# A decoder step on one core: the gate's decay made earlier on ScalarE, and the first loads and a polynomial put elsewhere

## The chip, the core and the metric

The kernel runs on one core of a Trainium2 chip. The metric is the device time of one execution in microseconds (us); lower is better. Engines are named as the profile names them: PE (TensorE products), PEld (TensorE weight loads), DVE (VectorE), ACT (ScalarE), POOL (GpSimd), SP (SyncE, which only issues DMAs here).

## What is computed

One layer of a hybrid decoder, for 256 prompt tokens and 8 x 4 sample tokens together, with the same weights. Cut to what matters here:

```
h  = rmsnorm(x, g)
xr, gr, q, kvc, kvs, kvw, g_nsa, g_m = split_in(h @ w_in)
# recurrent branch (RG-LRU)
xc = causal_dwconv(xr);  r, i = sigmoid(xc @ wa + ba), sigmoid(xc @ wx + bx)
log_a = -8 * r * softplus(-lam);  a = exp(log_a)
u = sqrt(-expm1(2 * log_a)) * (i * xc)
h_t = a_t * h_(t-1) + u_t;  y_rnn = h_t * gelu(gr)
# attention branch on q and the keys and values, then gates, w_out, a conv FFN, a last rmsnorm
```

The kernel writes t = tanh(r * 4 * softplus(-lam)), so that a = (1 - t) / (1 + t) = 2 / (1 + t) - 1 and sqrt(1 - a^2) = 2 sqrt(t) / (1 + t).

## The kernel before

All activations lie transposed: 128 features on the partitions, 288 tokens along the rows. A 128 x 1024 block of weights (8 tiles of 128 x 128) is loaded as `raw` and split into two parts in a shorter float format: `wh`, a copy made by ACT (line 161), and `wl`, the rest, made by DVE (line 162, on a few blocks by POOL). The activations are split in the same way into `hh` and `hl`. Each tile then takes three products of 288 columns (lines 179, 180, 181: wh by hh, wh by hl, wl by hh), so one block is 24 products. A block's work is called a step here.

`load_w` keeps the split two blocks ahead of the products: at the start of step i it puts the split of block i + 2 into the queues of ACT and DVE. There are 3 buffers for `wh`, 3 for `wl` and 4 for `raw`; the copy of block i + 2 waits until PE has finished with block i - 1. SP issues all weight loads in order. Every engine works through its queue strictly in program order, and that order is written by hand: `run` walks through units of steps, and `at(n, f)` puts the side function `f` behind step n of the walk.

Places that the change touches:

- The start (lines 285 to 340). `wake` sends 8 products of ones through PE. Then 8 chunks `c` of two feature blocks each are loaded: `x_load(c)` issues x (line 295) and the weights `wkc` (line 297). Chunk 0 goes in two halves, the others whole. The first half of chunk 0's weights is issued by ACT, all else by SP; the norm's vector `vec` (line 299) goes on SP behind the first half of x. `norm_in` makes `hh` on ACT (line 233, scaled by `vec`) and `hl` on DVE (line 234). For chunk 0 all products wh by hh come first, then wh by hl, then wl by hh (line 334); from chunk 1 on the three follow each other tile by tile. POOL issues the loads of the sample states `st` and `h0` (lines 358, 359) in its first microseconds.
- `r_lam1` (lines 392 to 401): a polynomial for softplus(-lam), 17 DVE instructions on 128 x 8 elements, the last of which writes `sp4`. It stands behind the norm's scale `dg` (lines 262 to 264) and ahead of the next two splits of weights on DVE. `xr_out(0)` (lines 374, 375) comes behind these splits and empties the PSUM bank that the unit after next fills.
- The recurrent branch runs as side work: for each of the 8 blocks j, `r_gate1` (sigmoids and tanh on ACT, then B = 1 + t on POOL) stands behind step 3j + 5 of the walk and `r_gate2` (B = 1 / B, line 496, DVE) behind 3j + 7. `r_sqrt` (ACT, line 499) stands behind steps 27 and 28, `r_gelu` (ACT, line 502) behind 29 and 30. `r_scan0(j)` behind step 28 + j and `r_scan1(j)` behind 29 + j are the scan stage: two DVE operations for u (lines 505, 506), then on ACT a = 2B - 1 in the place of B (line 507), then the scan itself on DVE (line 510). In that stage the units are the queries, and `unit_q` adds one DVE operation (line 447) at every second step.

Of the kernel before, what the change touches and what calls it, by code (L numbers as in the profile page):

```python
# [87 lines left out]
def body(ctx, tc, a, o):  # L88
# [196 lines left out]
    xcm, xp = pool("xp", side="right")  # L285
    acc = new_acc()
    acc2 = q_sb[:, 0:2]
    wake(psg(), 8)
    kz = [psb(), psb(), pst(), pso()]

    def x_load(c):
        xc = xp.tile([P, 2, N], F32, tag="xc", name="xc", bufs=8)
        raw = w_tiles(None)
        for ks in ((0, 1), (1, 2)) if c == 0 else ((0, 2),):
            nc.sync.dma_start(xc[:, ks[0]:ks[1]], a["x"][:, 2 * c + ks[0]:2 * c + ks[1]])
            first = c == 0 and ks[0] == 0
            (nc.scalar if first else nc.sync).dma_start(raw[:, 4 * ks[0]:4 * ks[1]], a["wkc"][c][:, 4 * ks[0]:4 * ks[1]])
            if first:
                nc.sync.dma_start(vec[:, V_GM:V_GM + KD], a["vec"][:, V_GM:V_GM + KD])
        if c == 5:  # L300
            nc.sync.dma_start(vec[:, KD:], a["vec"][:, KD:])
            nc.sync.dma_start(cs, a["cst"])
        return xc, raw
# [9 lines left out]
    for c in range(8):  # L313
        xc, raw = x_load(c)
        if c == 0:
            S.activation(warm, mhalf, AF.Copy)
        wh, wl = w_parts(raw)
        for k2 in range(2):
            k = 2 * c + k2
            norm_in(xc[:, k2], vcol(V_GM, k), hh[:, k], hl[:, k])  # L320
            if c == 0:
                split(wh[:, 4 * k2:4 * k2 + 4], wl[:, 4 * k2:4 * k2 + 4], raw[:, 4 * k2:4 * k2 + 4])
            elif k2 == 0:
                split(wh, wl, raw)
        if prev is not None and c > 1:
            V.tensor_add(acc2, acc2, prev)
        prev = x_squares(c, xc)
        for k2 in range(2):
            k = 2 * c + k2
            if c == 0:  # L330

                for n, (w, x) in enumerate(((wh, hh), (wh, hl), (wl, hh))):
                    for j in range(4):
                        T.matmul(kz[j][:, :N], w[:, 4 * k2 + j], x[:, k], start=k == 0 and n == 0, stop=False)
            else:
                for j in range(4):
                    mm3(kz[j][:, :N], wh[:, 4 * k2 + j], wl[:, 4 * k2 + j], hh[:, k], hl[:, k], False, k == KD - 1)
# [17 lines left out]
    B = rp.tile([P, RB, RW], F32, name="B")  # L355
    C = rp.tile([P, RB, RW], F32, name="C")
    orn = rp.tile([P, RB, 36], F32, name="orn")
    nc.gpsimd.dma_start(st, a["rcs"])
    nc.gpsimd.dma_start(h0, a["rh0"])
    rb = None  # L360

    def samp(t):
# [47 lines left out]
        pass  # L410
    rms_sum(qn, acc, True, True)
    dg = rms_diag(qn)
    r_lam1()
    g = unit(qx[1][:, :N], 2, hh, hl)
    next(g)
    qb = rms_bcast(dg)
# [78 lines left out]
    def r_gate2(j):  # L495
        V.reciprocal(B[:, j, :RC], B[:, j, :RC])

    def r_sqrt(j):
        S.activation(A[:, j:j + 2, :RC], A[:, j:j + 2, :RC], AF.Sqrt)

# [1 line left out]
        S.activation(gr[:, j:j + 2], gr[:, j:j + 2], AF.Gelu_apprx_tanh)  # L502

    def r_scan0(j):
        V.scalar_tensor_tensor(A[:, j, :RC], A[:, j, :RC], 2.0, B[:, j, :RC], op0=ALU.mult, op1=ALU.mult)
        V.tensor_mul(A[:, j, :RC], A[:, j, :RC], C[:, j, :RC])
        S.activation(B[:, j, :RC], B[:, j, :RC], AF.Identity, scale=2.0, bias=mone)

    def r_scan1(j):
        V.tensor_tensor_scan(C[:, j, :NP], B[:, j, :NP], A[:, j, :NP], 0.0, op0=ALU.mult, op1=ALU.add)  # L510
# [24 lines left out]
        side.setdefault(n, []).append(lambda: f(*args))  # L535

    for j in range(RB):
        for i, f in ((0, r_conv0), (1, r_conv1), (2, r_parts), (3, r_gate0), (4, r_gate1), (6, r_gate2)):
            at(3 * j + 1 + i, f, j)
        at(28 + j, r_scan0, j)  # L540
        at(29 + j, r_scan1, j)
        at(38 + j // 2, r_out0, j)
        at(39 + j // 2, r_out1, j)
    for i in range(4):
        at(27 + i // 2, r_sqrt, 2 * i)
        at(29 + i // 2, r_gelu, 2 * i)
# [709 lines left out]
```

## Time and profile before

| | us |
|---|---|
| median of 3 runs | 1673.66 (1673.54 to 1673.69) |
| profiled execution, its own time | 1674.1 |
| its span in the profile | 1672.3 |
| PE busy | 1645.1 (98%) |
| DVE busy | 1017.5 (61%) |
| ACT busy | 765.3 (46%) |

A busy PE in the profile is not a PE at its peak, since products are pipelined and their ends are modelled. Whether PE loses time is read from the starts of its products: in the undisturbed stretches one product of 288 columns starts 0.13 us behind the other. A stretch with fewer starts than that has lost time, and the row of the product that starts late names in brackets what it waited for.

### The profile page before, as it was taken

To read this page: it belongs to the slowest core of one execution; us is meant where nothing else is said; L and a number is where in the kernel's file an instruction comes from. 1 tells how busy PE (TensorE), PEld (TensorE's weight loads), DVE (VectorE), ACT (ScalarE), POOL (GpSimd) and SP (SyncE) were. 2 spreads that over 40 slices of the span, in tenths; PEclk is the share of its full clock that TensorE was granted. 3 is DMA by queue.
4 is the path that set the end of the run, shared out by engine and by line. 5 is a ranking of instruction groups with operands and counts; after the bars stand their busy time and mean duration, and the time that the engine had idled before them with its cause. 6 is when DMAs were issued, how large, how long until landed. Compare 5 with 4: busy or idle time off the path is not lost.

```text
span 1672.3 us, 31396 instructions
## 1 busy us (share of the span) xinstructions
PE 1645.1 (98%) x12722; PEld 1634.0 (98%) x12722; DVE 1017.5 (61%) x1544; ACT 765.3 (46%) x1091; POOL 247.2 (15%) x427
## 2 busy tenths in 40 slices
PE   9999999999999999999999999999999999999997
PEld 9999999899999999999999999999999999999997
DVE  6776867787775555666566556444456556654443
ACT  6555555565554444444444444333344444443332
POOL 0341100541440001330000000000000000001112
PEclk9999999999999999999999999999999999999999
DMA  7554585544556555555566655555555555555553
GB/s 269 178 170 132 156 295 175 157 144 153 171 169 212 164 174 167 167 169 159 172 200 205 198 163 167 172 171 165 167 163 165 175 163 166 174 175 175 157 175 107
DMA packets 88371, 290.79 MB, mean 174 GB/s; under 512 B 10178, under 2 KB 19154, under 8 KB 88098
## 3 DMA queue, kind: packets, MB, share of 16 engines
q1 hardware_dynamic: 85394, 276.73, 54.5%
q0 software_dynamic: 1968, 10.45, 1.9%
q8 instruction: 100, 1.64, 0.4%
q10 hardware_dynamic: 864, 1.59, 0.3%
q14 instruction: 45, 0.37, 0.1%
HBM read 284.02 MB, written 8.85 MB: 175 GB/s over the span
## 4 chain that ended last, share of the span: by engine, by line
PE 87%; DVE 6%; ACT 3%; issue 2%; POOL 1%; DMA 1%; SPq 0%; POOLq 0%; ACTq 0%; DVEq 0%
PE ps_g L179 28%; PE ps_g L181 27%; PE ps_g L180 27%; DVE wl L162 2%; PE ps_b L601 1%; DVE k L176 1%; ACT wh L161 1%; DVE mx L803 1%; DVE pr L806 1%; ACT pr L798 1%; DMA raw<-in_wkc_dram 0%; ACT k L175 0%; DVE pr L790 0%; POOL rest L859 0%; PE ps_b L181 0%
## 5 line engine op out<-in xcount | busy, mean ns | idle before, releaser
L162 DVE TENSOR_TENSOR wl<-raw,wh 128x1024 fp32r<-128x1024 f32 (+1 forms) x481 | 595.1, 1237 | 468.7 <-ACT wh L161 467.8
L161 ACT ACTIVATE wh<-raw 128x1024 fp32r<-128x1024 f32 (+1 forms) x497 | 523.4, 1053 | 362.7 <-PE ps_g L180 265.0
L179 PE MATMUL ps_g<-h2h,wh 128*128 128x288 f32 x1536 | 451.0, 294 | 0.0
L180 PE MATMUL ps_g<-h2l,wh 128*128 128x288 f32 x1536 | 450.8, 293 | 0.0
L181 PE MATMUL ps_g<-h2h,wl 128*128 128x288 f32 x1536 | 449.7, 293 | 0.0
L179 PE MATMUL ps_g<-hh,wh 128*128 128x288 f32 x1024 | 304.6, 297 | 1.2 <-DVE xr L375 0.7
L181 PE MATMUL ps_g<-hh,wl 128*128 128x288 f32 x1024 | 300.9, 294 | 4.3 <-DVE wl L162 4.3
L180 PE MATMUL ps_g<-hl,wh 128*128 128x288 f32 x1024 | 300.9, 294 | 0.0
L181 PEld LDWEIGHTS ps_g<-h2h,wl 128*128 128x128 f32 x1536 | 289.4, 188 | 0.0
L179 PEld LDWEIGHTS ps_g<-h2h,wh 128*128 128x128 f32 x1536 | 288.4, 188 | 0.1
L180 PEld LDWEIGHTS ps_g<-h2l,wh 128*128 128x128 f32 x1536 | 288.4, 188 | 0.1
L180 PE MATMUL ps_g<-gl,wh 128*128 128x288 f32 x768 | 225.4, 293 | 0.0
L179 PE MATMUL ps_g<-gh,wh 128*128 128x288 f32 x768 | 225.4, 293 | 0.0
L181 PE MATMUL ps_g<-gh,wl 128*128 128x288 f32 x768 | 224.8, 293 | 0.0
L181 PEld LDWEIGHTS ps_g<-hh,wl 128*128 128x128 f32 x1024 | 192.9, 188 | 5.9 <-DVE wl L162 5.9
L179 PEld LDWEIGHTS ps_g<-hh,wh 128*128 128x128 f32 x1024 | 192.4, 188 | 2.2 <-ACT wh L161 1.0
L180 PEld LDWEIGHTS ps_g<-hl,wh 128*128 128x128 f32 x1024 | 192.4, 188 | 0.2
L181 PEld LDWEIGHTS ps_g<-gh,wl 128*128 128x128 f32 x768 | 144.7, 188 | 0.0
L180 PEld LDWEIGHTS ps_g<-gl,wh 128*128 128x128 f32 x768 | 144.2, 188 | 0.0
L179 PEld LDWEIGHTS ps_g<-gh,wh 128*128 128x128 f32 x768 | 144.2, 188 | 0.0
L1065 POOL COPY fco<-u 128x2 f32<-128x2 f32 x48 | 8.8, 184 | 712.0 <-DVE u L1061 712.0
L1064 ACT ACTIVATE cv<-u,vec 128x304 f32<-128x304 f32 x48 | 30.8, 642 | 133.0 <-DVE u L1062 126.9
(328 smaller groups left out, 2101.6 us busy)
## 6 DMA issues: line engine op xcount, KB each, us to landing
raw<-in_wg_dram SPq DMA_DIRECT2D x96, 512.0 KB, 3.6
raw<-in_wu_dram SPq DMA_DIRECT2D x96, 512.0 KB, 4.1
raw<-in_wd_dram SPq DMA_DIRECT2D x96, 512.0 KB, 3.7
raw<-in_wga_dram SPq DMA_DIRECT2D x32, 512.0 KB, 3.6
raw<-in_wgb_dram SPq DMA_DIRECT2D x32, 512.0 KB, 3.6
raw<-in_wo_dram SPq DMA_DIRECT2D x32, 512.0 KB, 3.6
raw<-in_wxr_dram SPq DMA_DIRECT2D x16, 512.0 KB, 4.2
raw<-in_wgr_dram SPq DMA_DIRECT2D x16, 512.0 KB, 3.6
```

The lines of the kernel that those rows point to most:

```text
L161: S.activation(hi, src, AF.Copy)
L162: eng.tensor_sub(lo, src, hi.bitcast(F32))
L176: V.tensor_sub(part(2), r, part(1))
L179: T.matmul(out, wh, xh, start=first, stop=False)
L180: T.matmul(out, wh, xl, start=False, stop=False)
L181: T.matmul(out, wl, xh, start=False, stop=last)
L601: T.matmul(pc[:, 2 * k:2 * k + 272], w[:, l], f(x), start=lh == 0 and k == 0 and l == 0 and n == 0, stop=lh == 1 and k == 1 and l == 7 and ...
L798: S.activation(pr[:, s0:s1], pr[:, s0:s1], AF.Exp, scale=scale, bias=mx[:, i:i + 1], accum_out=sm[:, i:i + 1])
L803: V.tensor_scalar(sm[:, :n], sm[:, :n], 1e-30, None, op0=ALU.max)
L806: V.tensor_scalar(pr[:, s0:s1], pr[:, s0:s1], sm[:, i:i + 1], gates[:, i:i + 1], op0=ALU.mult, op1=ALU.mult)
L1064: S.activation(cv[:, :FC], u[:, 2:2 + FC], AF.Identity, scale=vcol(V_FW + 96, f), bias=vcol(V_FB, f))
L1065: G.tensor_copy(fco[:, f, 0:2], u[:, NP:NP + 2])
```

## The change

The copies of the first two half blocks of weights move from ACT to DVE (`tensor_copy`), and both halves are issued on ACT's DMA queue. The norm's vector is issued first on SP. Chunk 1 is loaded and split in halves as well. PE gets 9 products of ones instead of 8. The loads of `st` and `h0` move from POOL's queue to SP's, where they come behind chunk 7 in program order. `r_lam1` moves from ahead of the second unit to behind step 0 of the walk. A new side function `r_gate3(j)` makes a = 2B - 1 on ACT behind step 3j + 8, one step behind the reciprocal, so `r_scan0` finds a in B; it computes u from a + 1, which is 2 / (1 + t), with the same two DVE operations, and it no longer has an ACT operation.

```diff
-    wake(psg(), 8)
+    wake(psg(), 9)
+    nc.sync.dma_start(vec[:, V_GM:V_GM + KD], a["vec"][:, V_GM:V_GM + KD])
     def x_load(c):
...
-        for ks in ((0, 1), (1, 2)) if c == 0 else ((0, 2),):
-            nc.sync.dma_start(xc[:, ks[0]:ks[1]], a["x"][:, 2 * c + ks[0]:2 * c + ks[1]])
-            first = c == 0 and ks[0] == 0
-            (nc.scalar if first else nc.sync).dma_start(raw[:, 4 * ks[0]:4 * ks[1]], a["wkc"][c][:, 4 * ks[0]:4 * ks[1]])
-            if first:
-                nc.sync.dma_start(vec[:, V_GM:V_GM + KD], a["vec"][:, V_GM:V_GM + KD])
+        for k0, k1 in ((0, 1), (1, 2)) if c < 2 else ((0, 2),):
+            nc.sync.dma_start(xc[:, k0:k1], a["x"][:, 2 * c + k0:2 * c + k1])
+            (nc.sync if c else nc.scalar).dma_start(raw[:, 4 * k0:4 * k1], a["wkc"][c][:, 4 * k0:4 * k1])
...
+            if c == 0:
+                w4 = slice(4 * k2, 4 * k2 + 4)
+                V.tensor_copy(wh[:, w4], raw[:, w4])
+                norm_in(xc[:, k2], vcol(V_GM, k), hh[:, k], hl[:, k])
+                V.tensor_sub(wl[:, w4], raw[:, w4], wh[:, w4].bitcast(F32))
+                continue
             norm_in(xc[:, k2], vcol(V_GM, k), hh[:, k], hl[:, k])
-            if c == 0:
-                split(wh[:, 4 * k2:4 * k2 + 4], wl[:, 4 * k2:4 * k2 + 4], raw[:, 4 * k2:4 * k2 + 4])
+            if c == 1:
+                w4 = slice(4 * k2, 4 * k2 + 4)
+                split(wh[:, w4], wl[:, w4], raw[:, w4])
             elif k2 == 0:
                 split(wh, wl, raw)
...
-    nc.gpsimd.dma_start(st, a["rcs"])
-    nc.gpsimd.dma_start(h0, a["rh0"])
+    nc.sync.dma_start(st, a["rcs"])
+    nc.sync.dma_start(h0, a["rh0"])
...
     dg = rms_diag(qn)
-    r_lam1()
     g = unit(qx[1][:, :N], 2, hh, hl)
...
+    def r_gate3(j):
+        S.activation(B[:, j, :RC], B[:, j, :RC], AF.Identity, scale=2.0, bias=mone)
...
     def r_scan0(j):
-        V.scalar_tensor_tensor(A[:, j, :RC], A[:, j, :RC], 2.0, B[:, j, :RC], op0=ALU.mult, op1=ALU.mult)
+        V.scalar_tensor_tensor(A[:, j, :RC], B[:, j, :RC], 1.0, A[:, j, :RC], op0=ALU.add, op1=ALU.mult)
         V.tensor_mul(A[:, j, :RC], A[:, j, :RC], C[:, j, :RC])
-        S.activation(B[:, j, :RC], B[:, j, :RC], AF.Identity, scale=2.0, bias=mone)
...
-        for i, f in ((0, r_conv0), (1, r_conv1), (2, r_parts), (3, r_gate0), (4, r_gate1), (6, r_gate2)):
+        for i, f in ((0, r_conv0), (1, r_conv1), (2, r_parts), (3, r_gate0), (4, r_gate1), (6, r_gate2), (7, r_gate3)):
...
+    at(0, r_lam1)
```

What stands in ACT's queue in the scan stage, before (L499 and L502 are the square root and the gelu, L507 makes a, L161 copies weights to `wh`):

```order
L499 ACT_TABLE_LOAD
L499 ACTIVATE A<-A 128x2x312 x2
L161 ACTIVATE wh<-raw 128x1024
L507 ACTIVATE B<-B,mone 128x312
L499 ACTIVATE A<-A 128x2x312 x2
L161 ACTIVATE wh<-raw 128x1024
L507 ACTIVATE B<-B,mone 128x312
L502 ACT_TABLE_LOAD
L502 ACTIVATE gr<-gr 128x576 x2
L161 ACTIVATE wh<-raw 128x1024
L507 ACTIVATE B<-B,mone 128x312
L502 ACTIVATE gr<-gr 128x576 x2
```

ACT's queue at the same place now (L508 and L511 are the square root and the gelu, L505 makes a):

```order
L508 ACT_TABLE_LOAD
L508 ACTIVATE A<-A 128x2x312 x2
L161 ACTIVATE wh<-raw 128x1024
L508 ACTIVATE A<-A 128x2x312 x2
L161 ACTIVATE wh<-raw 128x1024
L505 ACTIVATE B<-B,mone 128x312
L511 ACT_TABLE_LOAD
L511 ACTIVATE gr<-gr 128x576 x2
L161 ACTIVATE wh<-raw 128x1024
L511 ACTIVATE gr<-gr 128x576 x2
L161 ACTIVATE wh<-raw 128x1024 x9
```

Of the eight operations that make a, seven now stand ahead of this stage; the last one is left in it, behind the reciprocal of block 7, and the copies of weights follow each other after that.

DVE's queue behind the norm's scale, before, from the last third of `r_lam1` on (the `lt` and `sp` rows):

```order
L396 TENSOR_SCALAR lt_458<-lt_457 128x8
L398 SCALAR_TENSOR_TENSOR lt_458<-lt_458,lt_457 128x8 x8
L399 SCALAR_TENSOR_TENSOR lt_458<-lt_458,lt_456 128x8
L400 TENSOR_SCALAR lt_453<-lt_453 128x8
L401 SCALAR_TENSOR_TENSOR sp_459<-lt_458,lt_453 128x8
L162 TENSOR_TENSOR wl<-raw,wh 128x1024 x2
L374 TENSOR_TENSOR xr<-ps_g,rb 128x256
L375 TENSOR_TENSOR xr<-ps_g,rb 128x8x4
```

And now, the same queue from the norm's scale `dg` on:

```order
L264 TENSOR_SCALAR dg<-cs,rt 128x128
L162 TENSOR_TENSOR wl<-raw,wh 128x1024 x2
L381 TENSOR_TENSOR xr<-ps_g,rb 128x256
L382 TENSOR_TENSOR xr<-ps_g,rb 128x8x4
L428 TENSOR_TENSOR kv_426<-ps_b,rb 128x288 x2
L428 TENSOR_TENSOR kv_426<-ps_t,rb 128x288
L428 TENSOR_TENSOR kv_426<-ps_o,rb 128x288
L381 TENSOR_TENSOR xr<-ps_g,rb 128x256
L382 TENSOR_TENSOR xr<-ps_g,rb 128x8x4
L162 TENSOR_TENSOR wl<-raw,wh 128x1024
L399 TENSOR_SCALAR lt_461<-lt_460 128x8
L400 RECIPROCAL lt_461<-lt_461 128x8
```

The polynomial, which begins in the last two rows, has passed three splits and the emptying of the first banks. SP's queue at the start, before:

```order
L295 DMA xc<-in_x_dram 128x288
L299 DMA vec<-in_vec_dram 128x16
L295 DMA xc<-in_x_dram 128x288
L297 DMA raw<-in_wkc_dram 128x512
L295 DMA xc<-in_x_dram 128x576
L297 DMA raw<-in_wkc_dram 128x1024
L295 DMA xc<-in_x_dram 128x576
L297 DMA raw<-in_wkc_dram 128x1024
```

And now:

```order
L291 DMA vec<-in_vec_dram 128x16
L298 DMA xc<-in_x_dram 128x288 x3
L299 DMA raw<-in_wkc_dram 128x512
L298 DMA xc<-in_x_dram 128x288
L299 DMA raw<-in_wkc_dram 128x512
L298 DMA xc<-in_x_dram 128x576
L299 DMA raw<-in_wkc_dram 128x1024
```

Both pieces end with the weights of chunk 2: the 8th issue on SP before, the 9th now.

## Rows read from the trace of the kernel before

**Rows 1.** The page: busy us (share of the span) and instructions of each engine.
```profile
PE 1645.1 (98%) x12722; PEld 1634.0 (98%) x12722; DVE 1017.5 (61%) x1544; ACT 765.3 (46%) x1091; POOL 247.2 (15%) x427
```

**Rows 2.** Stretches: length, busy (instructions) of PE, PEld, DVE, ACT, POOL; PEclk, DMA.
```profile
12.30:40.00 27.70, 27.70 (x213) 27.70 (x213) 22.28 (x34) 18.47 (x28) 0.00 (x0) 1.00 0.80 279
140.00:156.00 16.00, 16.00 (x125) 16.00 (x124) 9.41 (x12) 10.94 (x14) 1.41 (x1) 1.00 0.43 132
156.00:183.00 27.00, 22.22 (x152) 20.11 (x152) 18.81 (x29) 12.29 (x17) 0.00 (x0) 1.00 0.40 117
347.00:350.40 3.40, 3.33 (x19) 3.07 (x19) 2.30 (x7) 1.21 (x3) 0.00 (x0) 0.50 0.23 25
350.40:360.00 9.60, 9.60 (x92) 9.31 (x91) 9.43 (x20) 6.15 (x13) 5.91 (x4) 1.00 0.55 151
```

**Rows 3.** Scan stage in order of time: start, duration, what ran, [idle <- releaser].
```profile
164.03 0.56 ACT L507 ACTIVATE B<-B,mone 128x312 f32<-128x312 f32 x1 [2.63 <-DVE A L505]
164.49 1.05 ACT L161 ACTIVATE wh<-raw 128x1024 fp32r<-128x1024 f32 x1
165.57 1.23 DVE L162 TENSOR_TENSOR wl<-raw,wh 128x1024 fp32r<-128x1024 f32 x1 [1.05 <-ACT wh L161]
166.72 0.69 DVE L510 TENSOR_TENSOR_SCAN C<-B,A 128x256 f32<-128x256 f32 x1
166.85 0.40 PE L181 MATMUL ps_g<-hh,wl 128*128 128x288 f32 x1 [0.71 <-DVE wl L162]
167.32 0.46 DVE L505 SCALAR_TENSOR_TENSOR A<-A,B 128x312 f32<-128x312 f32 x1
167.81 0.48 DVE L506 TENSOR_TENSOR A<-A,C 128x312 f32<-128x312 f32 x1
170.49 0.45 DVE L447 SCALAR_TENSOR_TENSOR q_sb<-ps_g,rb 128x288 f32<-128x288 f32 x1
```

**Rows 4.** Who waited for whom from 140 to 183: total us, times, longest.
```profile
ACT B L507 <- DVE A L505: 19.0, 8, 2.6
```

**Rows 5.** The scan stage's beginning in order of time.
```profile
147.44 2.10 DVE L496 RECIPROCAL B<-B 128x312 f32<-128x312 f32 x1
152.97 1.28 ACT L502 ACT_TABLE_LOAD   x1
154.27 1.26 ACT L502 ACTIVATE gr<-gr 128x576 f32<-128x576 f32 x2
```

**Rows 6.** Around the polynomial, in order of time.
```profile
43.65 1.58 DVE L398 SCALAR_TENSOR_TENSOR lt<-lt,lt 128x8 f32<-128x8 f32 x8
45.63 2.36 DVE L162 TENSOR_TENSOR wl<-raw,wh 128x1024 fp32r<-128x1024 f32 x2
47.54 0.29 PE L181 MATMUL ps_g<-hh,wl 128*128 128x288 f32 x1
48.56 0.37 PE L179 MATMUL ps_g<-hh,wh 128*128 128x288 f32 x1 [0.73 <-DVE xr L375]
```

**Rows 7.** The start in order of time.
```profile
1.07 3.78 PE L280 MATMUL ps_g<-ones 128*128 128x128 f32 x16 [1.07 <-DVE mhalf L215]
4.30 0.41 SPq L297 DMA_DIRECT2D raw<-in_wkc_dram  x1
4.56 0.54 ACT L233 ACTIVATE hh<-xc,vec 128x288 fp32r<-128x288 f32 x1 [1.87 <-DMA vec<-in_vec_dram]
5.67 0.85 PE L334 MATMUL ps_b<-hh,wh 128*128 128x288 f32 x2 [0.81 <-ACT wh L161]
12.03 0.40 PE L181 MATMUL ps_b<-hh,wl 128*128 128x288 f32 x1 [0.73 <-DVE wl L162]
12.05 1.04 ACT L161 ACTIVATE wh<-raw 128x1024 fp32r<-128x1024 f32 x1
13.13 1.23 DVE L162 TENSOR_TENSOR wl<-raw,wh 128x1024 fp32r<-128x1024 f32 x1 [0.29 <-ACT wh L161]
```

**Rows 8.** DMA issued at 4.30: engine, count, size, us to landing.
```profile
raw<-in_wkc_dram SPq DMA_DIRECT2D x1, 512.0 KB, 7.4
```

## The prediction, made before the changed kernel ran

> **What bounds the kernel now.** I began with the page: PE is busy for 98% of the span [rows 1], the next engine for 61%, so the time is the sum of PE's products plus the stretches in which PE starts late. A time can only come out of those stretches. The second view is the table of stretches. From 12.3 to 40 us PE starts 213 products in 27.70 us [rows 2], which is 0.130 us each; that is the undisturbed pace, and one step of 24 products takes 24 x 0.130 = 3.12 us. From 156 to 183 us it starts only 152 in 27.00 us [rows 2]. At the undisturbed pace they need 152 x 0.130 = 19.8 us, so 7.2 us are lost there. The third view is the order of time inside that stretch, the fourth the order of time around the two other places which the change touches: the polynomial and the start.
>
> In the scan stage the rows show a ring. ACT's operation that makes a waits 2.63 us for DVE's first operation for u and starts at 164.03; behind it, at 164.49, comes the copy of a weight block; DVE's split of that block waits 1.05 us for the copy and starts at 165.57; PE's product on the split starts late at 166.85; behind the split DVE does the scan and the next block's u, whose first operation starts at 167.32 and releases ACT again [rows 3]. The two engines take turns: neither is full, and the ring is longer than a step of PE. The waits view counts eight such waits of ACT, 19.0 us in all [rows 4].
>
> **The change part by part.**
>
> *The decay on ACT one step behind the reciprocal.* Seven of the eight operations leave the ring and go to stretches in which ACT has room (18.47 of 27.70 us busy even at the start, [rows 2]); each lasts 0.46 us there (164.03 to 164.49, [rows 3]), on an ACT that keeps its copies two steps ahead, so I cost them at nothing; without that cover they would cost 7 x 0.46 = 3.2 us. The operations for u are the same two on DVE, with other operands. ACT then no longer waits for DVE, and the next thing that could be late is DVE's own queue. Its work in a step of the stage, from start to start: split 165.57 to 166.72, 1.15 us; scan 166.72 to 167.32, 0.60; the two operations for u, 0.49 and 0.48 [rows 3]. That is 2.72 us. At every second step the query's operation is added, at most 0.45 us [rows 3], which makes 3.17; the mean is 2.95, below PE's 3.12. So DVE holds the pace, with 5% to spare.
>
> The critical place is the beginning of the stage, where one reciprocal of 2.10 us is added on DVE (147.44 to 149.5), and the one operation left in the stage, that of block 7, waits for it on ACT. Queued behind it on ACT are the table load of 1.28 us, two gelu operations of 1.26 us together [rows 5], and then the copy of the next weight block, which DVE's split and two steps later PE wait for. Worked out: 149.5 + 0.46 + 1.28 + 1.26 = 152.5 for the start of that copy, 1.05 for the copy, 1.15 for the split [rows 3], so the split is ready at 154.7. PE wants it at about 156.5: from 140 to 156 it starts 125 products in 16.00 us, 0.128 us each, so none is late, and the loss begins behind that [rows 2]. That leaves 1.8 us of reserve, and after it DVE gains 0.17 us per step on PE. So I take the whole 7.2 us; the bounds are 4 (the reserve is not enough and 1.8 us, as much again, is lost at one step, with some of the short waits left) and 7.2.
>
> *The polynomial.* PE's last product ahead of the unit after next starts at 47.54 and the following one at 48.56, waiting for the emptied bank [rows 6]: 1.02 - 0.13 = 0.9 us lost. The eight middle operations of the polynomial last 1.58 us, so all 17 some 3 us, and only behind the splits (2.36 us) is the bank emptied [rows 6]. Without them the bank is empty some 2 to 3 us earlier (the copies on ACT set how much), before PE asks for it: gain 0.9. At the new place the same 3 us stand ahead of one split that has two steps, 6.2 us, of time. The copy, the wait for a buffer and the split take 2.5 us of that, so the split is some 1 to 2 us later than before and still 2 us early. Its result is first used by a tanh on ACT four steps later. Cost nothing; bounds for this part 0 to 0.9.
>
> *The start.* Three things happen. First, the first product: `hh` waits for the norm's vector until 4.56, then ACT copies the weights, and PE starts at 5.67 [rows 7]. With the copy on DVE next to `hh` on ACT, PE should start at about 5.1: `hh` takes 0.54 us [rows 7], and half of a DVE split of 1.23 us, as the nearest row for a half block [rows 7], is 0.6 us, both from about 4.5. The copy may cost less, which changes nothing, because `hh` is as long. Second, the clock: the products of ones run until 1.07 + 3.78 = 4.85 and leave a gap up to 5.67 [rows 7]; a ninth, an eighth of 3.78 us or 0.45, closes the gap if the first product comes at 5.1. Third, and this decides what remains of both: data. The chunk 2 weights are issued at 4.30 and land 7.4 us later [rows 8], at 11.7; ACT copies them from 12.05 for 1.04 us, DVE splits them from 13.13 for 1.23 us [rows 7], done at 14.36. PE's third product of chunk 1, the first that needs the split, starts at 12.03 [rows 7], so its chunk 2 wants the split at 12.03 + 24 x 0.130 = 15.15. However early PE starts, that product cannot start before the split is done: landing + 0.05 + 1.04 + 0.05 + 1.23. With the landing at 11.7 that is 14.05, a gain of 1.1; 128 KB of sample states no longer run ahead of it, which at the 279 GB/s of the nearest stretch [rows 2] is up to 0.45 us earlier, a gain of 1.55. On the other side the block is now the 9th issue on SP instead of the 8th; one issue is 0.41 us [rows 7]. I take 1.3; bounds 0.3 and 2.0. The states' loads now stand on SP ahead of the first `wxr` block, two issues of 0.4 us; PE has no late product from 12.3 to 40 [rows 2], so I cost that at nothing.
>
> The rows give the chunk 0 weights on ACT's queue no price of their own. The Trainium skill (DMA: Bandwidth & Descriptors, section "Issuing engines are not separate DMA queues") speaks against a gain there: transfers issued by different engines share the same DMA engines, and only the time of issuing is saved. By that rule the start would gain the 1.1 us of an unchanged landing, and the sum would be 0.2 us smaller.
>
> **The sum.** 7.2 + 0.9 + 1.3 = 9.4 us. The profiled execution took 1674.1 us for a span of 1672.3, so it would be 1664.7; the median of the runs lies 0.44 us below it, 1673.66, and becomes 1664.3. The bounds of the terms are 4 + 0 + 0.3 = 4.3 and 7.2 + 0.9 + 2.0 = 10.1, so 1669.4 to 1663.6.
>
> **The rivals.**
>
> *DVE becomes the limit.* For it: 2.95 us of work in a step of 3.12, and the reciprocal and the table load fall at the very beginning. Against it: the 1.8 us of reserve. If the reserve is eaten, PE is late by the rest of one reciprocal and one table load, 2 to 3 us, and the gain is 6.4 to 7.4: about 1667.
>
> *ACT is held all the same.* If the copies of weights still depend on DVE in the scan stage (a buffer, the last operation of block 7), the 7.2 us stay and only start and polynomial count: 1673.66 - 2.2 = 1671.5. Against it: in the new order nothing of DVE's scan stands ahead of the copies.
>
> *A drop of the clock goes.* From 347.0 to 350.4 PE's granted clock is 0.50, the level of 1.2 GHz, with 19 instructions in 3.40 us; in the next 9.6 us there are 92 [rows 2], so 19 would take 2.0, and the drop costs about 1.4 us. It follows a short idle stretch in the attention stage, which the change moves by 9 us without altering it. If the drop does not come again: 1664.3 - 1.4 = 1662.9. The Trainium skill (TensorE: Matmul & The Clock Gate, "Part 1: The HAM clock gate") says that the gate runs freely and does not start anew with the kernel, so that where it falls varies; by that rule this case is as likely as not, while the 0.15 us between the runs before speak for a fixed place.
>
> *Slower: more drops.* The same mechanism the other way. The attention stage from 300 us on has many short idle stretches, and one of them costs a drop now. Each more costs 1.4 us. From seven more on, 7 x 1.4 = 9.8, they outweigh the 9.4 us; with eight the time is 1673.7 - 9.4 + 11.2 = 1675.5. Against it: only one of them does it now.
>
> **How the numbers follow.** The forecast, all three terms within their bounds and the drop as it is, has 0.55: 1664.3. The drop gone has 0.2 (1662.9), DVE as limit 0.15 (1667), ACT held 0.06 (1671.5), slower by drops 0.02 (1675.5), and 0.02 for no change at all through two of these together. The range 1661.8 to 1667.3 takes in the first three with the start's bounds and leaves out about 0.15. About 0.2%, 3.3 us, is what a measurement of this kernel can tell from no change; faster than that, below 1670.3, are the first three: 0.91 with some of the fourth. Within it lie most of ACT held and of no change: 0.07. Slower 0.02.
>
> **What would show it.** Right: between 156 and 183 us, some 2 us earlier now, about 207 products in 27 us instead of 152, and no row of ACT's a that waits for DVE except one, of about 1.5 us, for the last reciprocal. At the bank no late product near 47. At the start a first product near 5.1 and the split of chunk 2 done near 13.8, with PE waiting for it. Wrong: late products on `wl` in the scan stage with DVE busy up to them (first rival), or waiting for ACT (second); a PEclk of 1.00 near 340, or more stretches of 0.50 (the last two).

## The result, and the profile after

The changed kernel takes 1664.68 us (median of 4 runs, 1664.50 to 1665.29) against 1673.68 for the kernel before beside it (1673.54 to 1674.96): a ratio of 0.9946, 95% interval [0.9934, 0.9959]. Its profiled execution took 1664.5 us for a span of 1662.7; that of before took 1674.1 for 1672.3, so the two traces differ by 9.6 us and the medians by 9.0.

The line of busy times, which answers to [rows 1], shows nearly the same work in a shorter span:

```profile
PE 1642.1 (99%) x12724; PEld 1633.7 (98%) x12724; DVE 1018.2 (61%) x1547; ACT 765.3 (46%) x1090; POOL 244.6 (15%) x425
```

To see where the time went, I compared the start of each PE product with that of the same product in the trace of before. The difference is called the **lead** here. It changes only where one of the two kernels is late or runs at the lower clock, so its steps are the terms of the sum:

| up to | lead, us | step, us | predicted |
|---|---|---|---|
| the first real product (5.67 before, 5.55 after) | 0.12 | 0.12 | 0.6 |
| behind chunk 2's third product, from 15 to 45 us after | 1.84 | 1.84 for the whole start | 1.3 |
| behind the emptied bank (48.56 before) | 2.85 | 1.0 | 0.9 |
| behind the scan stage | 10.17 | 7.3 | 7.2 |
| behind the attention stage | 9.87 | -0.3 | 0 |
| the end of the span | 9.6 | -0.27 | 0 |

**The scan stage.** The table of stretches, three of them shifted to the places that answer to [rows 2] (columns: stretch, its us, busy us and instructions of PE, PEld, DVE, ACT, POOL, then PEclk, DMA share, GB/s):

```profile
9.46:37.16 27.70, 26.97 (x205) 26.71 (x204) 21.82 (x35) 18.82 (x29) 5.18 (x8) 1.00 0.88 312
137.15:153.15 16.00, 16.00 (x125) 16.00 (x124) 11.05 (x15) 14.03 (x19) 1.82 (x2) 1.00 0.45 133
153.15:180.15 27.00, 27.00 (x208) 27.00 (x208) 25.13 (x47) 10.53 (x12) 4.46 (x12) 1.00 0.61 177
```

Where PE started 152 products in 27.00 us it now starts 208, the undisturbed pace. (The first stretch, 2.85 us earlier than in [rows 2], now takes in the wait at 13.33 and so counts 205.) DVE is busy for 25.13 of those 27.00 us, so it has little left. The order of time at the start of that stage shows the chain through the last reciprocal, and then two steps of DVE (columns: start us, duration us, engine, line, operation, out<-in, count, and in brackets the idle time before and what ended it):

```profile
144.92 2.10 DVE L502 RECIPROCAL B<-B 128x312 f32<-128x312 f32 x1
147.05 0.56 ACT L505 ACTIVATE B<-B,mone 128x312 f32<-128x312 f32 x1 [1.85 <-DVE B L502]
147.61 1.28 ACT L511 ACT_TABLE_LOAD   x1
150.07 1.04 ACT L161 ACTIVATE wh<-raw 128x1024 fp32r<-128x1024 f32 x1
151.15 1.23 DVE L162 TENSOR_TENSOR wl<-raw,wh 128x1024 fp32r<-128x1024 f32 x1 [1.21 <-ACT wh L161]
153.77 0.29 PE L181 MATMUL ps_g<-hh,wl 128*128 128x288 f32 x1
156.73 1.06 ACT L161 ACTIVATE wh<-raw 128x1024 fp32r<-128x1024 f32 x1 [2.08 <-PE ps_g L180]
156.78 1.22 DVE L162 TENSOR_TENSOR wl<-raw,wh 128x1024 fp32r<-128x1024 f32 x1
157.92 0.68 DVE L518 TENSOR_TENSOR_SCAN C<-B,A 128x256 f32<-128x256 f32 x1
158.52 0.46 DVE L514 SCALAR_TENSOR_TENSOR A<-B,A 128x312 f32<-128x312 f32 x1
159.01 0.48 DVE L515 TENSOR_TENSOR A<-A,C 128x312 f32<-128x312 f32 x1
159.41 1.22 DVE L162 TENSOR_TENSOR wl<-raw,wh 128x1024 fp32r<-128x1024 f32 x1
```

The ring of [rows 3] is gone: ACT's copy of 156.73 waits 2.08 us for PE to give a buffer back, not for DVE. DVE runs one step in 159.41 - 156.78 = 2.63 us without a pause. The split of 151.15 is done at 152.38, and PE first uses it at 153.77: a reserve of 1.4 us. The waits view (engine, line and what it waited for: us in all, times, longest), ACT from 134 to 175 us, answers to [rows 4]:

```profile
ACT wh L161 <- PE ps_g L180: 14.9, 8, 2.1
ACT B L505 <- DVE B L502: 3.4, 2, 1.8
```

**The start.** The order of time, answering to [rows 7]:

```profile
4.04 0.43 DVE L322 CAST wh<-raw 128x512 fp32r<-128x512 f32 x1 [2.91 <-DMA raw<-in_wkc_dram]
4.92 0.43 SPq L299 DMA_DIRECT2D raw<-in_wkc_dram  x1
4.96 1.13 ACT L233 ACTIVATE hh<-xc,vec 128x288 fp32r<-128x288 f32 x2 [1.78 <-DMA xc<-in_x_dram]
5.55 0.53 PE L341 MATMUL ps_b<-hh,wh 128*128 128x288 f32 x2 [0.76 <-ACT hh L233]
10.96 1.06 ACT L161 ACTIVATE wh<-raw 128x1024 fp32r<-128x1024 f32 x1 [1.25 <-DMA raw<-in_wkc_dram]
12.05 1.23 DVE L162 TENSOR_TENSOR wl<-raw,wh 128x1024 fp32r<-128x1024 f32 x1 [1.54 <-ACT wh L161]
13.33 0.40 PE L181 MATMUL ps_b<-hh,wl 128*128 128x288 f32 x1 [0.73 <-DVE wl L162]
```

`hh` no longer waits for the vector but for `x`, which landed at 4.9. The weights of chunk 2, issued at 4.92, were there at about 10.9, where ACT's wait for them ends, and PE waits 0.73 us for their split. The same product of chunk 2 in the trace of before stood here:

```profile
15.29 0.29 PE L181 MATMUL ps_b<-hh,wl 128*128 128x288 f32 x1
```

**The polynomial.** At the new place its operations lie between two splits; the bank had long been empty (`xr` from 44.54), and no product is late there:

```profile
44.54 0.42 DVE L381 TENSOR_TENSOR xr<-ps_g,rb 128x256 f32<-128x256 f32 x1
49.18 1.57 DVE L405 SCALAR_TENSOR_TENSOR lt<-lt,lt 128x8 f32<-128x8 f32 x8
51.18 1.23 DVE L162 TENSOR_TENSOR wl<-raw,wh 128x1024 fp32r<-128x1024 f32 x1
```

### The profile page after: what moved, and what is told of

Read it like the earlier page. It is cut to its first block, busy times and chain, and to the rows that moved or that the text cites. A ratio compares the mean times of both kernels' runs of the same rounds, so it can differ in the third digit from the quotient of the medians.

```text
span 1662.7 us, 31405 instructions
## 1 busy us (share of the span) xinstructions
PE 1642.1 (99%) x12724; PEld 1633.7 (98%) x12724; DVE 1018.2 (61%) x1547; ACT 765.3 (46%) x1090; POOL 244.6 (15%) x425
## 4 chain that ended last, share of the span: by engine, by line
PE 90%; DVE 5%; ACT 2%; DMA 1%; issue 1%; POOL 1%; POOLq 0%; SPq 0%; ACTq 0%; DVEq 0%
PE ps_g L179 29%; PE ps_g L181 28%; PE ps_g L180 28%; PE ps_b L610 1%; DVE k L176 1%; DVE wl L162 1%; ACT wh L161 1%; DVE pr L815 1%; DVE mx L812 1%; ACT pr L807 1%; DMA raw<-in_wga_dram 0%; DMA raw<-in_wkc_dram 0%; ACT k L175 0%; ACT k L173 0%; DVE pr L799 0%
## 5 line engine op out<-in xcount | busy, mean ns | idle before, releaser
L161 ACT ACTIVATE wh<-raw 128x1024 fp32r<-128x1024 f32 (+1 forms) x496 | 522.8, 1054 | 367.5 <-PE ps_g L180 277.0
```

Of the source, the lines that this page charges most:

```text
L161: S.activation(hi, src, AF.Copy)
```

## The experiments

Theory: three separate late places (ring in the scan stage, bank, start) were removed, each is worth what the table of leads shows, and they simply add. Rivals: they share a cause, or one of them is taken back elsewhere; and for the scan stage that DVE or ACT was close to being the next limit. Differences below a microsecond are read from the leads, since medians of one and the same kernel moved by half of one (1664.68 and 1664.22 for the changed kernel). The kernel before beside these runs took 1673.41 to 1674.34, so medians of different rows compare no better than that. Each lead comes from one profile of a kernel.

| kernel | median us (range, runs) | ratio to the kernel before |
|---|---|---|
| decay_alone | 1667.17 (1665.93 to 1667.57) | 0.9955 [0.9941, 0.9968] |
| start_alone | 1672.49 (1672.03 to 1674.22) | 0.9992 [0.9983, 1.0001] |
| poly_back | 1665.26 (1664.76 to 1668.14) | 0.9949 [0.9935, 0.9962] |
| extra_recip | 1665.34 (1664.48 to 1665.76) | 0.9951 [0.9937, 0.9965] |
| chunk1_whole | 1665.10 (1664.86 to 1667.22) | 0.9945 [0.9932, 0.9959] |
| second_half_sp | 1665.04 (1664.85 to 1665.52) | 0.9950 [0.9937, 0.9964] |
| second_half_sp_again | 1664.81 (1664.66 to 1664.99) | 0.9943 [0.9929, 0.9956] |
| states_pool | 1664.87 (1663.93 to 1665.50) | 0.9950 [0.9936, 0.9963] |
| wake8 | 1665.27 (1663.88 to 1666.28) | 0.9949 [0.9936, 0.9963] |
| halves2 | 1663.83 (1663.22 to 1665.23) | 0.9937 [0.9924, 0.9951] |
| halves2_again | 1663.83 (1663.58 to 1665.35) | 0.9939 [0.9925, 0.9952] |
| after_again | 1664.22 (1663.88 to 1664.37) | 0.9939 [0.9925, 0.9953] |

### The decay alone

The kernel before with only this:

```
+    def r_gate3(j):
+        S.activation(B[:, j, :RC], B[:, j, :RC], AF.Identity, scale=2.0, bias=mone)
 ...
-        V.scalar_tensor_tensor(A[:, j, :RC], A[:, j, :RC], 2.0, B[:, j, :RC], op0=ALU.mult, op1=ALU.mult)
+        V.scalar_tensor_tensor(A[:, j, :RC], B[:, j, :RC], 1.0, A[:, j, :RC], op0=ALU.add, op1=ALU.mult)
         V.tensor_mul(A[:, j, :RC], A[:, j, :RC], C[:, j, :RC])
-        S.activation(B[:, j, :RC], B[:, j, :RC], AF.Identity, scale=2.0, bias=mone)
 ...
-        for i, f in ((0, r_conv0), (1, r_conv1), (2, r_parts), (3, r_gate0), (4, r_gate1), (6, r_gate2)):
+        for i, f in ((0, r_conv0), (1, r_conv1), (2, r_parts), (3, r_gate0), (4, r_gate1), (6, r_gate2), (7, r_gate3)):
```

> The kernel before with the decay alone: a made by ACT one step behind the reciprocal, u from a + 1; start and polynomial as before. Theory (the scan stage is a ring of ACT and DVE, and the move cuts it): all 7.3 us of the scan stage come from this part, 1673.7 - 7.3 = 1666.4, with no late product between 140 and 190 us. Rival (part of that gain needs the earlier arrival that start and polynomial give): 1668 or more, with late products left in the stage.

Measured: 1667.17. The stretch of the scan stage, table of stretches:

```profile
154.00:181.00 27.00, 27.00 (x209) 27.00 (x208) 24.36 (x43) 11.47 (x13) 2.00 (x5) 1.00 0.55 165
```

The stage runs at full pace, and the lead grows by 7.3 us across it, as in the full change. The time lies 0.8 above the expectation. In the profiled execution (1667.46) there is another reason: PE lost 0.8 at the start, waiting for a chunk 0 block that landed late, with the start of the kernel before unchanged. Whether the other four runs (1665.93 to 1667.57) lost the same is not shown. Waits view, PE up to 60 us:

```profile
PE ps_b L334 <- ACT wh L161: 2.4, 2, 1.7
```

So the scan term stands by itself and needs neither of the other parts.

### The start alone

The kernel before with the vector first, the chunk 0 weights on ACT's queue and copied by DVE, chunk 1 in halves, the ninth product of ones and the states on SP; decay and polynomial as before.

> The changed kernel with decay and polynomial put back: the start's edits alone. Theory (the split of chunk 2 paces PE): first product near 5.55, chunk 2's wait at about 13.3, gain 1.84, time 1671.8. Rival (a gain at the start is given back in the ring of the scan stage, which waits anyway): no gain, 1673.6.

Measured: 1672.49, nearer to the expectation than to the rival; the ratio's interval alone would not exclude no change. In the trace the lead is 2.1 to 2.2 us from 35 to 300 us, crosses the scan stage unchanged and is 2.25 at the end. The ring is still there (waits view, ACT from 12 to 300 us):

```profile
ACT B L514 <- DVE A L512: 19.0, 8, 2.6
```

PE still waits for its splits in that stage, but the whole ring turns 2.2 us earlier than in the kernel before, so what PE gains at the start is not given back there.

### The polynomial put back

```
+    r_lam1()
     g = unit(qx[1][:, :N], 2, hh, hl)
 ...
-    at(0, r_lam1)
```

> The changed kernel with the polynomial back in its old place. Theory: the bank's wait comes back, 1.0 us, time 1665.7, a product late by about 0.9 near 46 us. Rival (the later stages take it up): 1664.7.

Measured: 1665.26, between the two expectations by its median. The trace decides: the lead over the changed kernel falls from +0.17 to -0.79 at one product and stays at -0.8 to the end, which is 0.95 us, and the late product is back (order of time):

```profile
46.51 0.37 PE L179 MATMUL ps_g<-hh,wh 128*128 128x288 f32 x1 [0.68 <-DVE xr L382]
```

### One more reciprocal: how large is the reserve

```
+        if j == RB - 1:
+            V.reciprocal(orn2, xr[:, j, 3:3 + RC])
         V.reciprocal(B[:, j, :RC], B[:, j, :RC])
```

`orn2` is a new tile that nobody reads.

> The changed kernel with work added: one more reciprocal of the same shape as the others, 2.1 us on DVE, into a tile that nobody reads, directly ahead of the reciprocal of block 7. It delays that reciprocal, behind it ACT's a, the table load, the gelu operations and the next weight copy, and DVE's split by the same 2.1 us, and stands in no other way. In the changed kernel the split that follows is done at 152.38 and PE wants it at 153.77, a reserve of 1.4 us. Theory (a reserve of 1.4 us and then nothing else): 2.1 - 1.4 = 0.7 us of late PE at one step, and the time 0.5 to 0.9 us above the changed kernel's. Rival one (the reserve is larger, since ACT and DVE take up the delay elsewhere): no late product, the same time within 0.2. Rival two (the reserve is no cushion, as the chain through both engines already ends just in time at a later step): 1.5 to 2.1 us above the changed kernel's, spread over several steps, as DVE gains only 0.17 us a step.

Measured: the lead over the changed kernel falls from +0.30 to -0.42 at one product and then keeps still to 300 us: 0.72 us. The rows in order of time:

```profile
144.61 2.10 DVE L504 RECIPROCAL orn<-xr 128x312 f32<-128x312 f32 x1
146.63 2.05 DVE L505 RECIPROCAL B<-B 128x312 f32<-128x312 f32 x1
152.81 1.23 DVE L162 TENSOR_TENSOR wl<-raw,wh 128x1024 fp32r<-128x1024 f32 x1 [1.21 <-ACT wh L161]
154.09 0.40 PE L181 MATMUL ps_g<-hh,wl 128*128 128x288 f32 x1 [0.46 <-DVE wl L162]
```

The split comes 1.96 us later than in the changed kernel when both are counted from their lead, PE is late by 0.72, so the reserve was 1.2 to 1.4 us, and what goes beyond it is paid once. The place that the prediction's first rival named is therefore real: with 2.1 us more on DVE it starts to cost, and with the change as it is it doesn't.

### Chunk 1 whole again

```
-        for k0, k1 in ((0, 1), (1, 2)) if c < 2 else ((0, 2),):
+        for k0, k1 in ((0, 1), (1, 2)) if c < 1 else ((0, 2),):
 ...
-            if c == 1:
-                w4 = slice(4 * k2, 4 * k2 + 4)
-                split(wh[:, w4], wl[:, w4], raw[:, w4])
-            elif k2 == 0:
+            if k2 == 0:
```

> The changed kernel with chunk 1 loaded, copied and split whole, as before the change; the vector first and the chunk 0 weights on ACT's queue stay. It tells apart what the start's 1.8 us come from. Theory (the halves of chunk 1 carry most of it): in the kernel before, PE's third product of chunk 1 waited for the whole block's split until 12.03 us, in the changed kernel it doesn't wait there and starts at 9.2. Whole again, the block lands near 9.0 to 9.6 (9.6 in the kernel before), its copy takes 1.06 us and its split 1.23, so that product starts at 11.3 to 12.0; chunk 2 follows 24 products or 3.1 us later at the earliest, at 14.5 to 15.2 instead of 13.33, and the time is 1.1 to 1.8 us above the changed kernel's. Rival (the order of the loads alone brings the gain): chunk 2's third product still starts by 13.6, time within 0.3 us.

Measured: the theory's sign, but less than its 1.1 to 1.8 us. The block landed at 8.6, earlier than its bound, and the first product on its split started at 11.03 after a wait (order of time):

```profile
8.66 1.06 ACT L161 ACTIVATE wh<-raw 128x1024 fp32r<-128x1024 f32 x1 [1.12 <-DMA raw<-in_wkc_dram]
11.03 0.40 PE L181 MATMUL ps_b<-hh,wl 128*128 128x288 f32 x1 [0.72 <-DVE wl L162]
11.05 1.05 ACT L161 ACTIVATE wh<-raw 128x1024 fp32r<-128x1024 f32 x1
14.28 0.29 PE L181 MATMUL ps_b<-hh,wl 128*128 128x288 f32 x1
```

Chunk 2's product starts at 14.28 instead of 13.33, and the lead from 33 us on is 0.84 smaller. So of the start's 1.84 us the halves of chunk 1 carry 0.84, and what is left of the start's edits the other 1.0, both read from one profile. The row of the kernel before for the same copy of chunk 1 shows where the 1.0 comes from:

```profile
9.66 1.06 ACT L161 ACTIVATE wh<-raw 128x1024 fp32r<-128x1024 f32 x1 [0.33 <-DMA raw<-in_wkc_dram]
```

The copy waits for the DMA in both kernels and begins 1.0 us earlier here (8.66 for 9.66), and PE's product on the split is 1.0 us earlier too (11.03 for 12.03). So the 1.0 is chunk 1's earlier landing, from the order and the queue of the first loads, and not DVE's taking over the copies of chunk 0. With the whole block ACT's copy of chunk 2 (11.05) has no wait for a DMA in front of it; it stands behind ACT's other work, as it did at 12.05 in [rows 7]. There PE was paced by chunk 1's landing, copy and split. In halves, the landing of chunk 2 is what is late next, which is the bound that the prediction named; it gave the halves that lead there no price.

### The second half of chunk 0 issued by SP

```
-            (nc.sync if c else nc.scalar).dma_start(raw[:, 4 * k0:4 * k1], ...)
+            (nc.scalar if c == 0 and k0 == 0 else nc.sync).dma_start(raw[:, 4 * k0:4 * k1], ...)
```

> The changed kernel with the second half of the chunk 0 weights issued by SP, as before the change, the first half still by ACT. Two readings of what the issuing engine is worth. By the rule that engines which issue share the same DMA engines, only the time of issuing moves: SP has one more issue of about 0.41 us ahead of the chunk 1 and chunk 2 loads, so chunk 2 lands up to 0.4 us later, its split is done at up to 13.7, and the time is up to 0.4 us above the changed kernel's. Rival (the bytes ahead of chunk 2 decide, not the issue): the landing stays at 10.9 plus or minus 0.1 and the time is the same within 0.1 us. A third outcome, the chunk 0 half landing so late that PE waits for it ahead of chunk 1, would show as a wait of PE for the second half block's split near 7 us.

> The second half of the chunk 0 weights issued by SP, once more. In its first profile ACT's copy of chunk 2 began about 0.4 us later than in the changed kernel's, which is one issue of SP; with the code unchanged that landing scattered by 0.3 us. Theory (one issue more on SP ahead of chunk 2): the copy of chunk 2 begins at 11.2 to 11.5 again, later than in the changed kernel's second profile, and the time is 0.3 to 0.4 us above it. Rival (scatter): it begins at 10.6 to 11.0 as well, same time.

Measured: chunk 2's copy began at 11.36 and 11.29 instead of 10.96 and 10.94, each time behind a wait for the DMA, and the lead is 0.40 and 0.32 smaller. First profile, order of time:

```profile
5.05 0.43 SPq L299 DMA_DIRECT2D raw<-in_wkc_dram  x1
11.36 1.06 ACT L161 ACTIVATE wh<-raw 128x1024 fp32r<-128x1024 f32 x1 [0.42 <-DMA raw<-in_wkc_dram]
```

The size, 0.3 to 0.4 us, is that of one issue on SP (0.43 us). In the second pair of profiles chunk 2 was issued 0.33 us later than in the changed kernel's (5.33 for 5.00), which is about the whole of it:

```profile
5.33 0.43 SPq L299 DMA_DIRECT2D raw<-in_wkc_dram  x1
```

In the first pair it was issued only 0.13 us later (5.05 for 4.92); that the rest came from the half block itself, which was issued later and so moved later, is argued, not shown. The scatter of the landing, 0.3 us, is of the same size. The first real product came half a microsecond earlier in these two profiles than in the changed kernel's (5.05 and 5.13 for 5.55), and the kernel was slower nevertheless: the first product does not pace the start. The Trainium skill (DMA: Bandwidth & Descriptors, "Issuing engines are not separate DMA queues") says that several issuing engines save only the time of issuing; the 0.3 to 0.4 us do not exceed that, so the runs agree with it.

### The states back on POOL's queue

```
-    nc.sync.dma_start(st, a["rcs"])
-    nc.sync.dma_start(h0, a["rh0"])
+    nc.gpsimd.dma_start(st, a["rcs"])
+    nc.gpsimd.dma_start(h0, a["rh0"])
```

> The changed kernel with the loads of the scan's first states and of the sample states back on POOL's queue, where they run beside the first chunks' loads. Theory of the prediction (they take bytes from the chunk 2 weights): 128 KB at 279 GB/s delay the landing by up to 0.45 us, from 10.9 to at most 11.35; the split of chunk 2 is done at up to 13.7 instead of 13.28, and the time is up to 0.4 us above the changed kernel's. Rival (the landing of chunk 2 does not depend on them): landing 10.9 plus or minus 0.1, the same time within 0.1 us; then the start's gain beyond 1.1 us comes from the order of the loads alone.

Measured: not later but 0.3 us earlier (order of time), with the states' bytes in flight beside it:

```profile
10.63 1.06 ACT L161 ACTIVATE wh<-raw 128x1024 fp32r<-128x1024 f32 x1 [0.41 <-DMA raw<-in_wkc_dram]
```

The extra reciprocal's kernel, whose start is that of the changed kernel, had this copy at 10.66, and two more with the same start had it at 10.70 (the start alone) and 10.79 (the polynomial put back), so 0.3 us is the scatter of the landing. The prediction's term of up to 0.45 us for these bytes falls: moving the states to SP gave nothing that can be seen.

### Eight products of ones

```
-    wake(psg(), 9)
+    wake(psg(), 8)
```

> The changed kernel with eight products of ones instead of nine. In the changed kernel the products of ones end at 4.79 us, the first real product starts at 5.55, and PE then reaches the split of chunk 2 before it is done (it waits 0.73 us for it, done at 13.28). Theory (the start is paced by the landing of chunk 2, not by PE): whatever the eighth and ninth product do to the moment at which the granted clock rises, PE arrives at that split earlier than it is done; the third product of chunk 2 starts at 13.3 plus or minus 0.2, and the time is 0 to 0.2 us from the changed kernel's. Rival (the ninth product carries part of the start's gain, by an earlier rise of the clock): PE is late by the low clock's excess, the third product of chunk 2 starts at 14 or later with no wait for the split, and the time is 0.7 us or more above the changed kernel's.

Measured, by the order of time at the product in question:

```profile
13.19 0.40 PE L181 MATMUL ps_b<-hh,wl 128*128 128x288 f32 x1 [0.72 <-DVE wl L162]
```

The start is as early as with nine, and the granted clock rose to 1.00 at 5.35 us in this profile, 4.13 in the changed kernel's. The theory holds: PE waits for the split with either, and the ninth product is worth nothing that can be seen. The median is 0.6 above the changed kernel's first; in the trace the lead is +0.15 up to 337 us and -0.93 behind it, and between the two lies one stretch at half clock (table of stretches):

```profile
336.40:343.20 6.80, 6.68 (x38) 6.32 (x38) 5.59 (x16) 4.04 (x8) 1.46 (x2) 0.50 0.36 98
```

### Chunk 2 in halves too

```
-            if c == 1:
+            if c in (1, 2):
                 w4 = slice(4 * k2, 4 * k2 + 4)
```

> The changed kernel with chunk 2's weights split in two halves as chunk 1's are (one load as now). Theory (PE waits 0.9 us for the split of chunk 2, which waits for the copy of the whole block): copy and split of the first half take 0.63 + 0.69 instead of 1.06 + 1.23, ready at about 12.3, before PE asks at 12.44; the wait goes and the time is 1664.7 - 0.9 = 1663.8. Rival (the wait moves to chunk 3, whose split is then late): 1664.7.

> Chunk 2's weights copied and split in halves as well, once more, beside the unchanged version on the same chip. The split of the first half is done 0.6 us after its copy of 0.5 us, instead of 1.23 after 1.05, so PE's third product of chunk 2 doesn't wait for it (no wait in the first profile of this kernel). Theory: the wait of 0.73 us of the changed kernel is gone whatever the landing, so the time is 0.4 to 0.9 us under that of the changed kernel. Rival: the difference of 0.85 us between the medians of the first runs was the scatter of the landing and of the clock's drops; the medians lie within 0.3 us.

> The changed kernel itself, once more, beside the two below on one chip: it gives the scatter of the landing of the chunk 2 weights and of the clock's drops with the code unchanged. Expected: about 1664.7 us; ACT's copy of chunk 2 begins between 10.6 and 11.0 us (10.96 in the first profile of this kernel); one or two drops of the clock, not at the same places as in the first profile.

Measured: 1663.83 twice, 0.85 and 0.39 under the changed kernel's medians. Only the second pair was run side by side; its difference lies at the edge of what the theory gave, the ranges of the runs overlap, and the ratios to the kernel before are the same (0.9939). In the traces the lead over the changed kernel is 0.62 and 0.70 from 33 us to the end, and no product of PE from 8 to 60 us waits. The two profiles had the copies of chunk 2 at different times:

```profile
11.00 0.63 ACT L161 ACTIVATE wh<-raw 128x512 fp32r<-128x512 f32 x1 [1.01 <-DMA raw<-in_wkc_dram]
11.96 0.62 ACT L161 ACTIVATE wh<-raw 128x512 fp32r<-128x512 f32 x1
```

and, in the second:

```profile
10.06 0.63 ACT L161 ACTIVATE wh<-raw 128x512 fp32r<-128x512 f32 x1 [0.45 <-DMA raw<-in_wkc_dram]
```

A copy that began 0.9 us earlier moved the lead by less than 0.1, so with halves the landing no longer sets PE's time. The changed kernel itself, run again, had the copy at 10.94 and one drop of the clock less.

## Point by point: the forecast of 1664.3 us and what came

The forecast held: 1664.68 where 1664.3 stood, within the range of 1661.8 to 1667.3, by the case that had the largest chance. That it came so close is partly luck: the three terms brought 10.17 us in the trace where the prediction had 9.4, and 0.57 us that it had not told went away again, 0.3 in the attention stage and 0.27 at the tail. The 0.3 is the second drop of the clock in the first profile; the second profile of the changed kernel, without that drop, does not lose it.

- **Scan stage, 7.2 predicted, 7.3 measured.** Each step came as told: 208 products where about 207 were expected, DVE at 2.63 us a step (2.72 told), no late product. The undisturbed pace of PE taken from another stretch gave the size of the loss, and the order of time said that DVE, the next thing in line, would just hold. Two details were off. The reserve behind the last reciprocal is 1.4 us, not 1.8. Counted from the lead of 2.85 us there, the reciprocal began 0.33 us later than in the kernel before, and the chain from it to the end of the split took 7.46 us instead of 7.26 (the a operation 0.56 instead of 0.46 among it), while PE asked for the split 0.1 us later than told. And ACT waits for its reciprocal at all eight blocks, not at one (waits view, ACT from 60 to 185 us):

```profile
ACT B L505 <- DVE B L502: 8.8, 8, 1.8
```

  That costs nothing: no product of PE is late there.
- **Polynomial, 0.9 predicted, 1.0 measured** (0.95 when it was put back). The cover that was named, two steps of time for the split at the new place, holds.
- **Start, 1.3 predicted, 1.84 measured.** This is the term that was mis-sized. Its last link held: PE waits for the split of chunk 2, and that split was done 2.4 us behind the landing, as told. The size was off by the landing, which was put at 11.25 to 11.7 and came at 10.9, earlier than both ends, although it was issued 0.6 us later. The bytes of the states, which were to explain 0.45 us of it, have no effect in the run that moves them back. The first product came at 5.55, not 5.1: with the vector first, `x` lands last (4.9), and the step that `hh` could begin near 4.5 had no row of its own; but the first product turned out not to pace the start. And the halves of chunk 1 had no price in the prediction, though the row of [rows 7] at 12.03 shows PE waiting for chunk 1's `wl`. Without the halves that wait stays, at 11.03, and the gain is 1.0, by the order and the queue of the first loads; the halves carry the other 0.84. Issuing one block of chunk 0 on ACT is worth 0.3 to 0.4 of the whole.
- **The clock.** In the attention stage the changed kernel has two stretches at half clock in one profile, and one in the other, where the kernel before had one. The prediction's price of a drop, 1.4 us, was the wrong size. The table of stretches and the waits of PE from 335 to 400 us, first in the changed kernel's first profile (the granted clock was 0.50 from 311.3 to 314.7 and from 338.6 to 342.1 us, so the stretches shown, which begin a little later, average 0.54):

```profile
311.60:315.00 3.40, 3.40 (x17) 3.40 (x16) 3.29 (x7) 3.40 (x7) 2.79 (x4) 0.54 0.37 112
338.90:342.30 3.40, 3.40 (x17) 3.40 (x16) 2.30 (x6) 3.20 (x6) 1.17 (x1) 0.54 0.52 154
```

```profile
PE ps_b L887 <- DVE ss L891: 1.7, 1, 1.7
PE ps_b L887 <- DVE k L176: 0.2, 1, 0.2
```

Then in its second profile, where the second drop didn't come:

```profile
338.90:342.30 3.40, 3.40 (x36) 3.31 (x35) 2.30 (x7) 3.25 (x6) 1.16 (x1) 1.00 0.54 154
```

```profile
PE ps_b L887 <- DVE ss L891: 1.7, 1, 1.7
PE ps_b L887 <- DVE k L176: 1.3, 2, 0.9
```

Without the drop PE is 1.5 us ahead at 345 us, and then waits 1.1 us more for DVE's `k`: the lead of the second profile over the first goes 0.05, 1.57, 0.35. This drop costs 0.3 us, not 1.4, because PE runs into a wait behind it anyway. The one at 311 us costs nothing in the end: the extra reciprocal's kernel, whose profile lacks it, gains 1.5 us on the changed kernel's there and has lost them again by 336 us. And the drop that the prediction priced, that of the kernel before at 347.0, is missing in the profile of the start alone: the lead grows there from 2.16 to 3.41 us and is back at 2.21 by 370 us, so that drop cost less than 0.1 us. Only the long one of 6.80 us cost more: 1.1 us beyond the changed kernel's drop at the same place. So the rival of 1662.9 was sized too far off, and the slower one would have needed over thirty drops of 0.3 us.

  Where the clock changes differed in the two runs of one kernel: the first drop came at 311.3 and 311.7 us, the second in one of them alone. This agrees with the Trainium skill (TensorE: Matmul & The Clock Gate, "Part 1: The HAM clock gate"), which says that the gate's timing runs freely and does not start anew with the kernel, so that the point of a transition varies. The prediction's remark that the close times of the runs before spoke for a fixed place carries little: at such a price, the times say next to nothing about the place.
- **The other rivals.** DVE as the limit did not come, but by 1.2 to 1.4 us only, as the extra reciprocal shows. ACT held all the same did not come: its waits in the scan stage are for PE's buffers, but for two (3.4 us) for reciprocals, and no product is late behind these.

Two things stay open: why chunk 2 lands sooner with later issue (only the halves of chunk 1, one issue and the states were taken apart), and the 0.27 us that the lead loses at the tail.

## What to carry to other kernels

Compare how many products the bound engine starts in equal stretches: the stretch with fewer gives the size of a loss before any cause is known, and here it gave it within 0.1 us. Where two engines with queues in order take turns, look for the one operation that sits in both queues and is ready earlier than it is issued; moving it out of the ring brought the whole loss here, since the fuller engine's step (2.6 to 3.0 us) still fitted into the bound engine's (3.12). At a kernel's start, ask which block the first wait is for, and look at that block's place among the loads and at its load, copy and split in halves before thinking about the load behind it: here the two gave 1.0 and 0.84 us.

## What the hardware showed that was not expected

- With the start's code unchanged, chunk 2's copy of the changed start began between 10.66 and 10.96 us in five profiles, and with chunk 2 in halves at 11.00 and 10.06. The second half of chunk 0 landed at 7.7 us in the kernel before and at 8.4 in the decay alone, whose start is the same. So loads at this kernel's start scatter by 0.3 to 0.9 us.
- The granted clock rose to 1.00 between 4.1 and 7.2 us in the profiles of the changed kernel and its variants, at 9.0 in that of the kernel before, and its drops in the attention stage (one or two, between 310 and 350 us) changed from run to run. Both cost little: the rise because PE waits for data behind it (with the extra reciprocal the clock rose at 6.9 us, and chunk 2's split was done 0.3 us earlier than in the changed kernel's first profile, where it rose at 4.1), the drop because PE waits behind it.
- DVE's copy of a 128x512 block into fp32r took 0.43 us, against 0.68 for the subtraction of the same shape and 0.63 for the copy on ACT.
